# Another issue order of the first stage of a hybrid decoder block: input and state-space input first, memory keys and values last

## The chip, the core and the metric

The kernel runs on one core of one Trainium2 chip. The metric is the device time of one execution in microseconds (us); lower is better. The time before the change is the median of three runs, 1627.50 us (1625.43 to 1628.37).

In what follows PE is TensorE (the matrix engine), DVE is VectorE, ACT is ScalarE, POOL is GpSimd and SP is the sync engine, which here issues every DMA. "L424" is line 424 of the kernel.

## What is computed

One decoder block over 1024 tokens of width 1024 in float32, with a memory of 256 tokens:

```
u = rms_norm(x, norm_mix);  proj = u @ w_in        # splits into u_ssm, q, k, v, f, gates
y_ssm = gelu(s5_ssm(u_ssm));  out_a = glu(y_ssm @ w_glu)
out_b = forgetting_attention(q, k, v, f) @ w_fox_o
h = x + (sigmoid(gate_a)*out_a + sigmoid(gate_b)*out_b) @ w_mix_out
h = h + memory_cross_attention(rms_norm(h), rms_norm(mem), w_mem_q, w_mem_kv, w_mem_o)
h = h + swiglu_ffn(rms_norm(h));  return rms_norm(h)
```

The change touches only the first stage. It makes three things: the normalised input u, turned so that channels lie on partitions; `u_ssm`, the first 512 columns of `proj`; and the keys and values of the memory, `rms_norm(mem) @ w_mem_kv`. None of the three pieces `u_ssm`, keys and values needs another; `u_ssm` is read by the second stage, the keys and values only by the cross-attention, far later.

## The kernel before

**Precision.** Each float32 operand is split into a high and a low part (`split`, L172: a ScalarE cast makes the high part, and VectorE subtracts it from the source for the low part, or GpSimd does where a flag says so). Every product is three matmuls, high by high, high by low and low by high (`mm3`, L161).

**The first stage** (`stage_in`, L327) is a string of steps, `ORDER_IN` (L40). A loop (L437) walks the string and calls one small function per step, so the string is the order in which the instructions are written down. Tokens are handled in tiles of 128: `m` and `n` are the two memory tiles, 0 to 7 the eight tiles of x. The letters are:

- `F t` fetches tile t (512 KB, L344); `G0` and `G1` fetch the gains of the memory norm and the input norm, spread over all partitions (L348). All share eight buffers of the tag `xt`.
- `Q t` squares and sums a tile on ScalarE (L353). `R` makes the reciprocal root (L182): for a pair of x tiles it is eleven small VectorE instructions, for a memory tile one of them is on GpSimd. `S t` scales the tile (L212 on VectorE; with a `g`, L209 on ScalarE and L210 on GpSimd).
- `T t b` turns half a tile by four TensorE transposes (L218); `E t b` splits the result into high and low parts of u or of the memory (L173, L174).
- `D i` fetches weight block i (512 KB, L377): 0 to 3 are the columns of the keys, 4 to 7 rows of the values, 8, 9, a and b the four column blocks of `w_in` that give `u_ssm`. `W i` splits it. There are two raw buffers and four pairs of split buffers, in rotation: a fetch waits until an earlier split has read its buffer, a split until an earlier product has used its pair.
- `K h` and `k h` are the product and the split of one head's keys (24 matmuls of 256 columns), `V` and `v` the same for the values (4 times 12 matmuls of 512 columns, all four into two PSUM banks). When they are done, they are stored in DRAM (`kv_d`, L396 and L411).
- `U q h` is one of eight products of `u_ssm` (24 matmuls of 512 columns): column block q for half h of the tokens. Half 0 needs x tiles 0 to 3, half 1 tiles 4 to 7. `u q h` copies the result out (L421) and, after half 1, stores it by eight DMAs to `u_d` (L424).
- `L0` issues the fourteen small loads of the state-space parameters (L1028 to L1046), `L1` turns them (L1048 to L1059). `P` is one piece of the tables made from them (`prepare`, L1061), nearly all VectorE.
- `X24` is 24 matmuls on the identity, to warm TensorE up (L231).

The tiles of `us` and of the keys and values share four buffers (tag `kv`). All tiles of the stage lie in a pool called `xin`, which is given back when the stage is written down; the second stage's pool, `qp`, is placed where it lay (L312 to L315).

**The second stage** (`stage_ssm`, L441) interleaves 32 gate products (24 matmuls of 512 columns each, two to a 512 KB weight block of `w_in`, L149) with the state-space work of four groups of channels. For each group: `weights` (L1157) makes power tables on GpSimd and VectorE (it begins at L1175 and ends with the doubling steps of L1207 to L1209), `turn_weights` (L1217) turns them on TensorE (L1224, L1230) and places them by seven DMAs, `states` (L1241) reads `u_d`, multiplies (L1252) and scans on VectorE, `out` (L1284) multiplies (L1294, L1295) and takes the gelu on ScalarE (L1298). The first group's `turn_weights` stands before the fifth gate product, its `out` before the tenth.

**What sets the order.** The program is written down in the order above, but each engine's queue is drawn up at build time by the framework's planner. It ranks instructions by the order of writing and may let a later one pass an earlier one that it expects to be waiting. Within a queue the hardware runs in order: an engine whose first instruction waits holds up those behind it. SP's queue holds all DMA issues.

Of the kernel before, what the change touches and what calls it, by code (L numbers as in the profile page):

```python
# [37 lines left out]
RSLOT_LATE = (0, 1, 2, 3, 4, 4, 5, 5, 6, 6, 7, 7)  # L38

ORDER_IN = """  # L40
G0 Fm Qm Fn D1 X24 Qn Rm D0 Sm F1 G1 Tm0 Rn Em0 Sn Tn0 F0 Tm1 W0 Q0 Tn1 En0 F2 Q1 W1g En1 Em1 K0 D2 F3 K1 R0
S0 T00 T01 k0 E00 Q2 W2g D3 E01 D4 S1 T10 Q3 W3 k1 D5 K3 K2 W4 E10 W5 D6 R1 k2 T11 k3 S2 F4 Q4 V0 F5 S3g T30
E11 D7 Q5 F7 T20 R2 T21 E21 E20 S4 E30 W6 W7 T40 V1 D8 S5 E40 W8 T31 V2 L0 T41 E31 V3 D9 Db T50 F6 Q6 v T51 W9
E51 U00 Da Q7 L1 E41 u00 R3 S6 Wa T60 E50 S7 T61 T70 Wbg E61 U10 E60 P0 U20 u10 T71 E70 E71 u20 P1 U21 U11 U30
P2 u30 U31 u11 u31 U01 u21 P3 P4 P5 u01
"""


# [1614 lines left out]
```

## Time and profile before

| | us |
|---|---|
| median of three runs | 1627.50 |
| the profiled execution's own time | 1627.33 |
| its span, first to last instruction | 1625.6 |
| TensorE busy in the span | 1548.8 |
| TensorE's first matmul of the gates (second stage) | 111.53 |
| TensorE's last work of the second stage | about 328 |
| mean granted TensorE clock | 0.976 |

The profile is of one execution. Its span is 1.7 us shorter than the execution's time. A row of the time line gives the start, the length, the engine, the line and operation, what it writes and reads and, in brackets, the idle time of the engine ahead of it and what ended it. A row of stretches gives, for each, its length, each engine's busy time with the number of instructions, the granted TensorE clock (1.00 is full speed), the busy share of the DMA engines and GB/s. A row of waits reads "who <- for whom: us in total, times, longest".

### The profile page before, as it was taken

To read this page: it belongs to the slowest core of one execution; us is meant where nothing else is said; L and a number is where in the kernel's file an instruction comes from. 1 tells how busy PE (TensorE), PEld (TensorE's weight loads), DVE (VectorE), ACT (ScalarE), POOL (GpSimd) and SP (SyncE) were. 2 spreads that over 40 slices of the span, in tenths; PEclk is the share of its full clock that TensorE was granted. 3 is DMA by queue.
4 is the path that set the end of the run, shared out by engine and by line. 5 is a ranking of instruction groups with operands and counts; after the bars stand their busy time and mean duration, and the time that the engine had idled before them with its cause. 6 is when DMAs were issued, how large, how long until landed. Compare 5 with 4: busy or idle time off the path is not lost.

```text
span 1625.6 us, 20551 instructions
## 1 busy us (share of the span) xinstructions
PE 1548.8 (95%) x7313; PEld 1271.5 (78%) x7313; DVE 1022.2 (63%) x1850; ACT 646.4 (40%) x1169; POOL 257.2 (16%) x339
## 2 busy tenths in 40 slices
PE   7799599999899989999999989999999999899997
PEld 6588588899677768888888777888888888688886
DVE  6645554514678786764355698767666776555555
ACT  6322233322566654222235565333333333244342
POOL 2107465100111112310001210001000000000001
PEclk8899899999899999999999999999999999899999
DMA  7655567742321463544303145444554454795642
GB/s 262 124 87 103 52 123 128 144 85 32 50 54 47 118 163 94 166 130 143 91 12 102 56 182 188 149 155 158 164 169 151 160 164 160 263 380 193 196 156 104
DMA packets 226102, 221.77 MB, mean 136 GB/s; under 512 B 50872, under 2 KB 159512, under 8 KB 226000
## 3 DMA queue, kind: packets, MB, share of 16 engines
q1 hardware_dynamic: 226000, 220.47, 48.2%
q8 instruction: 57, 0.93, 0.2%
q14 instruction: 45, 0.37, 0.1%
HBM read 154.06 MB, written 64.32 MB: 134 GB/s over the span
## 4 chain that ended last, share of the span: by engine, by line
PE 77%; DVE 9%; DMA 6%; ACT 3%; POOL 2%; issue 2%; SPq 0%; POOLq 0%; DVEq 0%; ACTq 0%
PE mm L766 14%; PE mm L163 7%; PE mm L164 7%; PE mm L165 7%; PE pv L766 7%; PE mm L905 4%; PE sc L905 3%; PE sc L766 3%; PE sc L163 3%; PE sc L164 3%; PE sc L165 3%; PE pv L905 3%; DMA raw<-in_w_in_dram 2%; PE misc L905 2%; DVE wlo L174 1%
## 5 line engine op out<-in xcount | busy, mean ns | idle before, releaser
L174 DVE TENSOR_TENSOR wlo<-raw,whi 128x1024 fp32r<-128x1024 f32 (+2 forms) x126 | 133.6, 1062 | 190.4 <-ACT whi L173 178.1
L173 ACT CAST whi<-raw 128x1024 fp32r<-128x1024 f32 (+2 forms) x129 | 116.0, 903 | 302.5 <-DMA raw<-in_w_in_dram 79.0
L163 PE MATMUL mm<-uh,whi 128*128 128x512 f32 x344 | 140.3, 408 | 0.3 <-DVE mc L1482 0.3
L165 PE MATMUL mm<-uh,wlo 128*128 128x512 f32 x344 | 138.0, 401 | 0.0
L164 PE MATMUL mm<-ul,whi 128*128 128x512 f32 x344 | 137.7, 400 | 0.0
L174 DVE TENSOR_TENSOR ol<-or,oh 128x1024 fp32r<-128x1024 f32 x73 | 88.7, 1224 | 72.9 <-ACT oh L173 72.5
L173 ACT CAST oh<-or 128x1024 fp32r<-128x1024 f32 x73 | 76.8, 1053 | 107.0 <-PE pv L905 40.5
L798 POOL TENSOR_TENSOR g<-a,c 128x512 f32<-128x512 f32 x22 | 35.3, 1606 | 390.2 <-ACT a L797 390.2
L165 PEld LDWEIGHTS mm<-uh,wlo 128*128 128x128 f32 x344 | 66.6, 193 | 13.7 <-DVE wlo L174 0.2
L163 PEld LDWEIGHTS mm<-uh,whi 128*128 128x128 f32 x344 | 67.1, 195 | 13.0 <-DVE mc L1482 0.6
L164 PEld LDWEIGHTS mm<-ul,whi 128*128 128x128 f32 x344 | 66.9, 194 | 11.8
L192 POOL TENSOR_TENSOR r<-ms,mhalf 128x1 f32<-128x1 f32 x26 | 17.4, 671 | 369.2 <-DVE ms L188 360.7
L1514 POOL TENSOR_TENSOR pl<-pf,ph 128x512 fp32r<-128x512 f32 (+1 forms) x32 | 36.9, 1152 | 235.8 <-DVE ph L1513 221.9
L1511 ACT ACTIVATE pf<-sc 128x512 f32<-128x512 f32 (+1 forms) x96 | 46.3, 489 | 49.1 <-DVE sc L1507 34.1
L766 PE MATMUL pv<-S3h,we 128*128 128x512 f32 x176 | 58.2, 390 | 1.0 <-ACT S3h L173 1.0
L905 PE MATMUL mm<-oh 128*128 128x512 f32 x106 | 41.5, 391 | 0.0
L905 PE MATMUL mm<-ol,oh 128*128 128x512 f32 x106 | 41.5, 391 | 0.0
L905 PE MATMUL mm<-oh,ol 128*128 128x512 f32 x106 | 41.5, 391 | 0.0
L1517 DVE TENSOR_TENSOR pl<-pf,ph 128x512 fp32r<-128x512 f32 (+2 forms) x64 | 36.4, 571 | 7.8 <-ACT ph L1516 7.2
L165 PE MATMUL sc<-uh,wlo 128*128 128x512 f32 x104 | 40.6, 390 | 0.5 <-DVE wlo L174 0.5
L163 PE MATMUL sc<-uh,whi 128*128 128x512 f32 x104 | 40.8, 393 | 0.0
L163 PE MATMUL mm<-yh,whi 128*128 128x512 f32 x104 | 40.8, 392 | 0.0
(574 smaller groups left out, 4553.5 us busy)
## 6 DMA issues: line engine op xcount, KB each, us to landing
or<-c_d SPq DMA_DIRECT2D x77, 256.0 KB
raw<-in_w_ffn_in_dram SPq DMA_DIRECT2D x22, 512.0 KB
rawb<-in_w_ffn_in_dram SPq DMA_DIRECT2D x22, 512.0 KB
wo<-in_w_ffn_out_dram SPq DMA_DIRECT2D x22, 512.0 KB
c_d<-g SPq DMA_DIRECT2D x44, 256.0 KB
t_d<-wo SPq DMA_DIRECT2D x44, 256.0 KB
or<-t_d SPq DMA_DIRECT2D x44, 256.0 KB
raw<-in_w_in_dram SPq DMA_DIRECT2D x20, 512.0 KB
```

The lines of the kernel that those rows point to most:

```text
L163: T.matmul(ps, lh, rh, start=first, stop=False)
L164: T.matmul(ps, lh, rl, start=False, stop=False)
L165: T.matmul(ps, ll, rh, start=False, stop=last)
L173: self.A.copy(hi, src)
L174: (self.G if pool_lo else self.V).tensor_sub(lo, src, f32(hi))
L192: self.G.tensor_tensor(out=r, in0=v, in1=self.mhalf[:, 0:n], op=ALU.pow)
L766: T.matmul(ps, l_[:, k, :], r_, start=first and k == 0 and i == 0, stop=k == 3 and i == 2, skip_group_check=True)
L798: G.tensor_mul(g[:, 512:], a1, c1)
L905: T.matmul(ps, l_[:, gi], r_[:, 512:], start=n < 3 and p == 0 and k == 0 or n == 7 and p == 0 and k == 0, stop=p == NP - 1 and k == 2, ski ...
L1511: A.activation(pf[:, off:], ps[:, off:], AF.Exp)
L1514: G.tensor_sub(pl[:, off:], pf[:, off:], f32(ph[:, off:]))
L1517: V.tensor_sub(pl[:, off:], pf[:, off:], f32(ph[:, off:]))
```

## The change

Only the string changes; each step is in both, once, with the same flags but for two weight blocks (1 and 2), whose low parts go from GpSimd to VectorE.

```diff
 ORDER_IN = """
-G0 Fm Qm Fn D1 X24 Qn Rm D0 Sm F1 G1 Tm0 Rn Em0 Sn Tn0 F0 Tm1 W0 Q0 Tn1 En0 F2 Q1 W1g En1 Em1 K0 D2 F3 K1 R0
-S0 T00 T01 k0 E00 Q2 W2g D3 E01 D4 S1 T10 Q3 W3 k1 D5 K3 K2 W4 E10 W5 D6 R1 k2 T11 k3 S2 F4 Q4 V0 F5 S3g T30
-E11 D7 Q5 F7 T20 R2 T21 E21 E20 S4 E30 W6 W7 T40 V1 D8 S5 E40 W8 T31 V2 L0 T41 E31 V3 D9 Db T50 F6 Q6 v T51 W9
-E51 U00 Da Q7 L1 E41 u00 R3 S6 Wa T60 E50 S7 T61 T70 Wbg E61 U10 E60 P0 U20 u10 T71 E70 E71 u20 P1 U21 U11 U30
-P2 u30 U31 u11 u31 U01 u21 P3 P4 P5 u01
+F0 F1 G1 X24 F2 F3 D8 Q0 Q1 R0 F4 F5 S0 T00 E00 T01 F6 E01 S1 D9 T10 E10 T11 E11 Q2 Q3 R1 S2 T20 W8 E20 T21 E21 F7
+S3g T30 E30 T31 E31 Q4 Q5 R2 U00 Da S4 T40 E40 W9 T41 E41 S5 T50 E50 T51 E51 U10 u00 Q6 Q7 R3 Db S6 T60 E60 T61 E61
+Wa L0 S7 T70 E70 T71 E71 U20 u10 Fm Fn G0 Wbg U30 u20 L1 D0 U01 u30 P0 D1 u01 W0 Qm Qn Rm Sm U11 u11 P1 W1 Tm0 Em0
+Tm1 Em1 D2 P2 U21 u21 W2 Rn Sn P3 Tn0 En0 Tn1 En1 D3 P4 U31 u31 P5 W3 D4 K0 k0 D5 K1 k1 W4 D6 K2 k2 W5 D7 K3 k3 W6
+V0 W7 V1 V2 V3 v
 """
```

In the new string x is fetched, normalised and turned first, with the eight products of `u_ssm` following as their tiles and weights come (first half 0 of all four blocks, then half 1). The memory tiles are fetched behind them, and the four key products and the four value products end the stage. `us` is stored before the keys and values are computed, and the stage's last stores are those of the keys and values.

## The prediction

> **What bounds the kernel now.** I read the page first, then the table of stretches, then TensorE's waits, then the chain of waits around its largest gap.
>
> ```profile
> span 1625.6 us, 20551 instructions
> PE 1548.8 (95%) x7313; PEld 1271.5 (78%) x7313; DVE 1022.2 (63%) x1850; ACT 646.4 (40%) x1169; POOL 257.2 (16%) x339
> ```
> ```profile
> core 0: us, PE busy (x) PEld busy (x) DVE busy (x) ACT busy (x) POOL busy (x), PEclk, DMA share, GB/s
> 0.00:53.10 53.10, 39.03 (x225) 32.32 (x225) 34.59 (x86) 29.61 (x55) 11.84 (x15) 0.90 0.75 228
> 53.10:111.50 58.40, 52.27 (x221) 42.41 (x222) 37.47 (x159) 16.33 (x31) 4.13 (x1) 0.91 0.53 98
> 111.50:175.00 63.50, 59.54 (x291) 50.49 (x290) 32.56 (x36) 16.00 (x26) 41.15 (x85) 0.97 0.51 97
> 175.00:199.00 24.00, 11.12 (x49) 8.59 (x48) 12.03 (x17) 4.10 (x6) 8.45 (x15) 0.83 0.62 55
> 199.00:328.00 129.00, 129.00 (x646) 110.42 (x647) 66.54 (x93) 47.19 (x79) 54.07 (x103) 0.97 0.71 129
> ```
> TensorE (PE) is the bound: 1548.8 of 1625.6 us. Its missing 76.8 us lie partly here: 53.10+58.40−39.03−52.27 = 20.2 us before 111.5, where the gates' matmuls start, 4.0 us up to 175, 12.9 us up to 199, and none from there to 328. So a reordered first stage can win only at these gaps, and slow clock beside them (0.90 and 0.91 granted).
>
> ```profile
> PE pv L1224 <- ACT m L1298: 12.4, 1, 12.4
> PE misc L218 <- DVE ul L174: 3.6, 2, 3.3
> PE misc L218 <- DVE xt L212: 3.0, 1, 3.0
> ```
> ```profile
> 91.35 25.79 SPq L424 DMA_DIRECT2D u_d<-us  x32
> 119.34 0.99 POOL L1175 TENSOR_TENSOR w<-ld_re,bb_re 128x448 f32<-128x448 f32 x1 [41.02 <-DMA u_d<-us]
> ```
> ```profile
> 180.09 1.15 DVE wlo L174
> 181.25 13.54 DMA raw<-in_w_in_dram
> 198.21 0.61 ACT m L1298
> 198.95 1.94 PE pv L1224 x8
> ```
> The second fence is the key. GpSimd's first instruction on the state-space tables (L1175) sat idle 41.0 us and ran at 119.34, when the last store of `us` had landed: the second stage's tiles lie where the first stage's lay, so its table chain starts only when the first stage's last tile is free. The third fence is the end of that chain: tables, scans, a late weight split, a load of 13.54 us, ScalarE's gelu, and TensorE back at 198.95. Tables to restart is 198.95−119.34 = 79.6 us. TensorE stands idle before that restart and is full after it, so **the start of the table chain, not the start of the gates, carries to the end.** What I must find is when it starts after the change.
>
> **The change, part by part.** 140 steps change places; none is added or removed. Two weight splits (W1, W2) move their low part from GpSimd to VectorE, 2×1.22 us by the row below, which I cost at nothing: they fall under U, where TensorE has 43 us of work and VectorE only waits to serve it; without that cover they would delay K by as much. The work of the stage goes: x tiles and norms, state-space input U (8 products), memory K (4) and V (4). The sum follows TensorE to the end of V, then the last store.
>
> *DMA supply.* Rows of ScalarE, each released by a load:
> ```profile
> 6.61 1.06 ACT L353 ACTIVATE junk<-xt 128x1024 bf16<-128x1024 f32 x1 [4.53 <-DMA xt<-in_mem_dram]
> 8.02 1.06 ACT L353 ACTIVATE junk<-xt 128x1024 bf16<-128x1024 f32 x1 [0.27 <-DMA xt<-in_mem_dram]
> 152.46 1.05 ACT L173 CAST whi<-raw 128x1024 fp32r<-128x1024 f32 x1 [6.86 <-DMA raw<-in_w_in_dram]
> 158.39 1.05 ACT L173 CAST whi<-raw 128x1024 fp32r<-128x1024 f32 x1 [4.88 <-DMA raw<-in_w_in_dram]
> ```
> The second and third 512 KB of the queue landed at 6.61 and 8.02: 1.4 us per tile of 4 KB rows. Two 512 KB blocks of `w_in` (512-byte pieces) landed 5.93 us apart: four times slower. New queue: F0 at 5.2, F1 6.6, G1 8.0, F2 9.4, F3 10.8, D8 16.7, F4 to F6 by 20.9, D9 26.8, F7 28.2, Da 34.1, Db 40.0 (estimates from those two spacings). The Trainium skill's DMA: Bandwidth & Descriptors, Specifications, puts line rate at pieces of 512 B and more; by it all four blocks would be there about 18 us sooner and the 3 us stall below would go (1617.3). The trace disagrees, and I go by 5.93.
>
> *Start of U.* U00 needs tiles 0 to 3 turned and W8 split. VectorE's prices:
> ```profile
> 17.69 0.17 DVE L190 TENSOR_SCALAR ms<-ss 128x2 f32<-128x2 f32 x1 [0.35 <-ACT junk L353]
> 19.86 2.48 DVE L212 SCALAR_TENSOR_TENSOR xt<-xt,r,gain 128x1024 f32<-128x1024 f32 x2
> ```
> ```profile
> L174 DVE TENSOR_TENSOR wlo<-raw,whi 128x1024 fp32r<-128x1024 f32 x11 | 13.5, 1223 | 11.9 <-ACT whi L173 11.9
> L174 DVE TENSOR_TENSOR ul<-misc,uh 128x256 fp32r<-128x256 f32 x16 | 6.7, 419 | 0.1
> L174 POOL TENSOR_TENSOR wlo<-raw,whi 128x1024 fp32r<-128x1024 f32 x3 | 10.6, 3529 | 45.7 <-ACT whi L173 45.7
> ```
> A pair's root took 19.86−17.69 = 2.17 us, a scaling 1.24, a quarter tile's low part 0.42, a weight split 1.22. Two roots, three scalings (the fourth is GpSimd's), 16 low parts and one split are 4.3+3.7+6.7+1.2 = 15.9 us. They begin when F1 is squared, 6.6+1.3 = 7.9. So U00 starts at **24** (bounds 20, if short gaps overlap, and 30, if each tile's TensorE, ScalarE, VectorE round trip is exposed).
>
> *TensorE's work from there.*
> ```profile
> 100.42 0.39 PE L165 MATMUL mm<-uh,wlo 128*128 128x512 f32 x1
> 111.30 0.39 PE L165 MATMUL mm<-uh,wlo 128*128 128x512 f32 x1
> 23.00 0.28 PE L165 MATMUL mm<-mh,wlo 128*128 128x256 f32 x1
> 24.06 0.28 PE L165 MATMUL mm<-mh,wlo 128*128 128x256 f32 x1
> 54.97 0.63 PE L163 MATMUL mm<-uh,whi 128*128 128x512 f32 x1
> 57.10 0.63 PE L165 MATMUL mm<-uh,wlo 128*128 128x512 f32 x1
> 37.70 0.60 PE L218 MATMUL misc<-ident,xt 128*128 128x128 f32 x4
> ```
> From 100.42 to 111.30 are 48 matmuls: 0.227 us each at full clock; the narrow ones 9 in 1.06, 0.118 each; cold ones (54.97 to 57.10) 5 in 2.13, 0.43 each. U is 8×24×0.227 = 43.5 us; K 96×0.118 = 11.3; V 48×0.227 = 10.9. Twelve groups of four transposes (x tiles 4 to 7, memory) at 0.4 (0.60 less the overlap with the next matmul) are 4.8, the state-space loads' five small ones 1.3. A cold start, as at 53.95 to 57.5, costs 10×(0.43−0.23) = 2.0, because TensorE has only scattered transposes to do after its 24 warm-up matmuls. TensorE: Matmul & The Clock Gate in the Trainium skill, Part 4, says that transposes do not count as busy for the clock; by that those 2.0 us are certain, and if transposes did keep the clock the result would be 1618.3; no row here isolates it.
>
> *Weights.* W9 is ready at 26.8+2.2 = 29 and Wa at 36.3, before U10 and U20 need them (about 32 and 37.5). Db at 40.0 plus 1.05 of ScalarE plus 3.53 of GpSimd gives 44.6 against about 44: up to 1 us. The small state-space loads are free to slip ahead of Db:
> ```profile
> 33.03 0.80 SPq L1039 DMA_DIRECT2D craw<-in_c_re_dram  x1
> 38.22 0.43 SPq L377 DMA_DIRECT2D raw<-in_w_mem_kv_dram  x1
> 39.80 4.26 SPq L1039 DMA_DIRECT2D craw<-in_c_re_dram  x3
> 44.10 3.96 SPq L1039 DMA_DIRECT2D craw<-in_c_im_dram  x4
> ```
> Seven of them held the queue 8.2 us. I take 3 us for the stall, from 0 to 8. End of U: 24+43.5+2.0+4.8+1.3+3.0 = **78.6**. W0 to W3 have landed by then, since U01 to U31 free their slots one by one 5.4 us apart. K and V: 22.2 plus 2 for weights just in time, so V ends at **102.8** (111.5 ended U before, with K and V behind it already).
>
> *The last store.* New: the last tiles of the stage are V's, split (two casts, two subtractions, 2.0 us) and stored by two 512 KB DMAs after V, where `us` stores lie under K and V. How long these take to land, no row shows there: from below, the last `us` store, whose row ends at 117.14, had landed by 119.34, 2.2 us; from above 5.9 of a gate weight ahead in the queue plus 2×1.4 plus 2.2 = 10.9. I take 7.5, nearer the upper, because gate weights are fetched in that very stretch. The table chain starts at 102.8+2.0+7.5 = **112.3** against 119.3: 7.0 us sooner.
>
> *Sum.* 1627.33 (the profiled execution; its span 1625.6 and 1.7 around it) − 7.0 = **1620.3**. The median, 1627.50, is the same to 0.2. The gates start 8.7 us sooner but gain nothing of their own: the 16.9 us of gaps from 111.5 to 199 go on ending with the table chain, 79.6 us after its start. All later stages keep their order and shift as one.
>
> **The rivals.**
> *Slower: V's weights arrive one by one.* The sync engine's issues leave in order, and 32 `us` stores, each set of eight waiting for a U, now stand among D2 to D7.
> ```profile
> 10.98 1.99 ACT L173 CAST whi<-raw 128x1024 fp32r<-128x1024 f32 x2 [1.80 <-DMA raw<-in_w_mem_kv_dram]
> 43.18 1.05 ACT L173 CAST whi<-raw 128x1024 fp32r<-128x1024 f32 x1 [1.06 <-DMA raw<-in_w_mem_kv_dram]
> ```
> In before, eight key and value blocks took 43.18−10.98 = 32.2 us from first to last cast, with two raw buffers and nothing of `us` between. At that pace, plus 1.2 for the last split and 2.7 for the last product, K and V last 36.1 instead of 24.2: +11.9, the chain starts at 124.2, and the time is 1627.3+4.9 = **1632.2**. It decides once K and V last over 31.2 us. Against it: four of the eight are loaded under U.
>
> *No change: the state-space loads go ahead of Db.* The planner already let them pass a weight (the fetch at 38.22 stands ahead of them in the order string, yet the load at 33.03 left before it). 8.2 us ahead of Db instead of 3, and another cold start of 2.0: +7.2, **1627.5**. So the written order need not be the order of the queues.
>
> *The second gap closes.* ScalarE's cast for a late weight stood ahead of gelu; if the planner, from another start, puts gelu first, the 12.4 us wait goes: **1607.9**. For it: the next three groups show no such gap (129.0 of 129.0 busy). Against: chain and gates stand nearly as before to each other, 9.5 us apart instead of 7.8.
>
> **How the numbers follow.** Forecast 1620.3, chance 0.40; its own range 1614 to 1626. Slower rival 0.30, no change 0.15, gap closed 0.15. Faster or slower by 0.2% is 3.3 us, about what a measurement here can tell from none. Faster: 0.37+0.15 = 0.52; same: 0.03 of the forecast, 0.02 of the slower rival and 0.11 of the unchanged one, 0.16; slower: 0.28+0.04 = 0.32. The bounds move the forecast by −4 to +6 (start of U), −3 to +5 (stall), −5.3 to +3.4 (store). For 8 in 10 the range is 1606 to 1637: from just under the closed gap to 5 over the slower rival.
>
> **What would show it.** U's first matmul near 24 and its last near 79, the fourth product waiting on a weight by some 3 us; K and V in one run to about 103; L1175 near 112, released by a store of keys and values; TensorE's restart 79.6 us behind it; full from there. Wrong if L1175 is released by something else or its distance to the restart changes, if a cast for D4 to D7 stalls ScalarE with TensorE waiting, or if stages after 328 of before differ in length by more than 2 us.

## The result, and the profile after

The changed kernel takes 1641.44 us in the median of six runs (1638.11 to 1645.01), the kernel before 1627.58 beside it: ratio 1.0079, 95% interval 1.0062 to 1.0097. It is 13.9 us slower, where 7.2 us faster was forecast. The profiled execution of after took 1645.01, the longest of the six, so its later positions are up to 3.6 us late. Of all executions in this document one stood far out, 8734 us, in the run "woven, tables first": its ratio leaves it out, and its median is 1627.38 without it.

The page of after, its head (us, share of the span, instructions):

```profile
span 1643.2 us, 20562 instructions
...
PE 1553.7 (95%) x7313; PEld 1274.2 (78%) x7313; DVE 1018.8 (62%) x1852; ACT 646.6 (39%) x1169; POOL 250.9 (15%) x337
```

TensorE's idle time grew from 76.8 to 89.5 us. Here is the first stage of after cut at its own marks: the first product of U, the first of K, the last of V, the first of the gates.

```profile
core 0: us, PE busy (x) PEld busy (x) DVE busy (x) ACT busy (x) POOL busy (x), PEclk, DMA share, GB/s
0.00:39.78 39.78, 13.93 (x60) 10.61 (x60) 20.03 (x60) 19.68 (x37) 4.49 (x12) 0.67 0.74 179
39.78:93.31 53.53, 52.23 (x242) 42.50 (x242) 41.86 (x171) 15.82 (x34) 4.28 (x3) 0.96 0.45 104
93.31:128.40 35.09, 28.83 (x145) 24.35 (x143) 10.15 (x13) 7.96 (x11) 0.00 (x0) 0.85 0.49 124
128.40:134.47 6.07, 0.12 (x1) 0.00 (x1) 0.02 (x1) 1.10 (x2) 0.00 (x0) 0.90 0.46 98
```

U began at 39.78, not 24; it lasted 53.5 us, as forecast (54.6); K and V lasted 35.1, not 24.2, at a granted clock of 0.85; and the gates waited 6.1 us for their first weight. The row on which the forecast turned, GpSimd's first instruction on the tables, and the row of ScalarE that tells what let it go (the tables' tiles lie where the keys' and values' lay):

```profile
146.52 0.62 ACT L1213 COPY r<-R 128x512 f32<-128x512 f32 x1 [1.60 <-DMA kv_d<-kv]
```
```profile
146.79 0.99 POOL L1175 TENSOR_TENSOR w<-ld_re,bb_re 128x448 f32<-128x448 f32 x1 [93.20 <-DMA raw<-in_w_in_dram]
```

So the chain starts 27.5 us later than before (119.34) and 34.5 later than forecast (112.3): 15.8 at the start of U, 10.9 in K and V, 8.9 between V's end and the chain (18.4 for 9.5), less 1.1 in U. Yet the end moved only half as far. TensorE's waits after the first stage in after, with the last gate's sigmoid (L453, first to last start) of both kernels, before first:

```profile
PE pv L1294 <- DMA Tt<-W: 5.0, 1, 5.0
PE pv L1295 <- DVE St L1281: 4.0, 2, 3.7
...
PE pv L1252 <- ACT F L1225: 1.2, 1, 1.2
```
```profile
L453 ACT ACTIVATE gs<-mm x19: 588/597/620, 122.6 to 342.8; 128x512 f32<-128x512 f32 x19
```
```profile
L453 ACT ACTIVATE gs<-mm x19: 591/599/602, 153.7 to 358.4; 128x512 f32<-128x512 f32 x19
```

The 12.4 us for the gelu (L1298) is gone. From the chain's start to the last sigmoid it is 211.6 us (358.4−146.8), where before had 223.5. Slower by 27.5, shorter by 11.9: 15.6 us, and 13.9 by the medians.

### The profile page after: what moved, and what is told of

The parts are those of the page before. It is cut to its first block, busy times and chain, and to the rows that moved or that the text cites. A ratio compares the mean times of both kernels' runs of the same rounds, so it can differ in the third digit from the quotient of the medians.

```text
span 1643.2 us, 20562 instructions
## 1 busy us (share of the span) xinstructions
PE 1553.7 (95%) x7313; PEld 1274.2 (78%) x7313; DVE 1018.8 (62%) x1852; ACT 646.6 (39%) x1169; POOL 250.9 (15%) x337
## 4 chain that ended last, share of the span: by engine, by line
PE 76%; DVE 8%; DMA 6%; ACT 3%; POOL 3%; issue 2%; SPq 1%; POOLq 0%; DVEq 0%; ACTq 0%
PE mm L766 14%; PE pv L766 7%; PE mm L163 7%; PE mm L165 7%; PE mm L164 7%; PE mm L905 4%; PE sc L905 3%; PE sc L766 3%; DMA raw<-in_w_in_dram 3%; PE sc L163 3%; PE sc L165 3%; PE sc L164 3%; PE pv L905 3%; PE misc L905 2%; DVE wlo L174 1%
## 5 line engine op out<-in xcount | busy, mean ns | idle before, releaser
L174 DVE TENSOR_TENSOR wlo<-raw,whi 128x512 fp32r<-128x512 f32 (+2 forms) x128 | 133.9, 1049 | 172.2 <-ACT whi L173 164.9
L164 PE MATMUL sc<-ul,whi 128*128 128x512 f32 x104 | 41.0, 394 | 0.0
```

Source lines behind the costliest of these rows:

```text
L164: T.matmul(ps, lh, rl, start=False, stop=False)
L174: (self.G if pool_lo else self.V).tensor_sub(lo, src, f32(hi))
```

## The experiments

All runs in one table. "Chain" is the first instruction of L1175, or what stands on that line; +9.9 and +19.8 are the repeats that were added behind it. The ratio is to the kernel before on the same chip.

| run | median us | ratio, 95% | U00 | chain | last sigmoid | chain to sigmoid |
|---|---|---|---|---|---|---|
| before | 1627.58 | | 53.95 | 119.3 | 342.8 | 223.5 |
| after | 1641.44 | 1.0079 (1.0062–1.0097) | 39.78 | 146.8 | 358.4 | 211.6 |
| W8 late | 1641.92 | 1.0075 (1.0059–1.0091) | 40.41 | 145.5 | 357.0 | 211.5 |
| D8, W8 late | 1639.83 | 1.0059 (1.0044–1.0074) | 31.16 | 142.8 | 354.6 | 211.8 |
| key copies on VectorE | 1640.10 | 1.0075 (1.0055–1.0096) | 40.19 | 143.6 | 355.1 | 211.5 |
| key and value weights as rows | 1640.65 | 1.0070 (1.0055–1.0085) | 39.65 | 142.5 | 354.7 | 212.2 |
| three queues | 1634.39 | 1.0044 (1.0027–1.0060) | 40.98 | 136.8 | 348.9 | 212.1 |
| three queues, D8 late | 1630.67 | 1.0017 (1.0006–1.0028) | 31.70 | 131.9 | 343.0 | 211.1 |
| value stores by GpSimd | 1644.00 | 1.0101 (1.0081–1.0121) | 40.37 | 148.5 | 360.0 | 211.5 |
| woven | 1631.21 | 1.0013 (1.0003–1.0022) | 33.49 | 133.4 | 347.1 | 213.7 |
| woven, tables first | 1627.65 | 1.0000 (0.9989–1.0011) | 34.38 | 132.0 | 345.7 | 213.7 |
| after, chain +9.9 | 1649.47 | 1.0131 (1.0115–1.0148) | 39.51 | 142.7+9.9 | 362.7 | 210.1 |
| before, chain +9.9 | 1624.20 | 0.9968 (0.9955–0.9981) | 54.12 | 120.1+9.9 | 338.5 | 208.5 |
| before, chain +19.8 | 1632.04 | 1.0025 (1.0015–1.0035) | 54.76 | 119.8+19.8 | 346.3 | 206.7 |
| before, one low part on GpSimd | 1623.92 | 0.9969 (0.9958–0.9981) | 53.87 | 120.1 | 337.0 | 216.9 |

Positions in one execution scatter, and this bears on small differences in the table. In "after, chain +9.9" nothing of the first stage was changed, yet its chain starts 4.1 us sooner than in the profile of after (142.7 for 146.8), and its keys and values last 33.4 us for 35.1, at a granted clock of 0.91 in place of 0.84 from K's first product to V's. So a chain that starts 4 us sooner, or keys and values that are 2 us shorter, are not clear of this scatter by themselves.

### The start of U

In after, rows of ScalarE, VectorE and TensorE show why U00 came late:

```profile
9.56 1.06 ACT L353 ACTIVATE junk<-xt 128x1024 bf16<-128x1024 f32 x1 [2.48 <-DMA xt<-in_x_dram]
...
18.65 1.04 ACT L173 CAST whi<-raw 128x1024 fp32r<-128x1024 f32 x1 [6.65 <-DMA raw<-in_w_in_dram]
```
```profile
13.22 0.16 DVE L197 SCALAR_TENSOR_TENSOR rt<-rt,ms 128x2 f32<-128x2 f32 x1
19.73 1.23 DVE L174 TENSOR_TENSOR wlo<-raw,whi 128x1024 fp32r<-128x1024 f32 x1 [6.35 <-ACT whi L173]
20.87 0.15 DVE L198 SCALAR_TENSOR_TENSOR r<-rt,r 128x2 f32<-128x2 f32 x1
```
```profile
25.92 1.09 PE L218 MATMUL misc<-ident,xt 128*128 128x128 f32 x4 [12.48 <-DVE rt L196]
...
39.78 1.65 PE L163 MATMUL mm<-uh,whi 128*128 128x512 f32 x3 [3.33 <-ACT uh L173]
```

The root of tiles 2 and 3 is cut in two: VectorE stands 6.35 us before the low part of the first w_in block, whose load lands at 18.65, and the rest of the root waits behind it. The first run writes that split later.

```diff
-F0 F1 G1 X24 F2 F3 D8 Q0 Q1 R0 F4 F5 S0 T00 E00 T01 F6 E01 S1 D9 T10 E10 T11 E11 Q2 Q3 R1 S2 T20 W8 E20 T21 E21 F7
-S3g T30 E30 T31 E31 Q4 Q5 R2 U00 Da S4 T40 E40 W9 T41 E41 S5 T50 E50 T51 E51 U10 u00 Q6 Q7 R3 Db S6 T60 E60 T61 E61
+F0 F1 G1 X24 F2 F3 D8 Q0 Q1 R0 F4 F5 S0 T00 E00 T01 F6 E01 S1 D9 T10 E10 T11 E11 Q2 Q3 R1 S2 T20 E20 T21 E21 F7 S3g
+T30 E30 T31 E31 Q4 Q5 R2 W8 U00 Da S4 T40 E40 W9 T41 E41 S5 T50 E50 T51 E51 U10 u00 Q6 Q7 R3 Db S6 T60 E60 T61 E61
```

> The changed kernel with one step moved: W8, the split of the first block of w_in, is written just ahead of U00 in place of between the tiles' turns. Theory (queue order): the split's cast (18.65) and subtraction (19.73) stand in the two engines' queues behind a block that lands at 18.65, and hold up the tiles' roots and casts by about 6 us each; without that U00 starts at 26 to 32 instead of 39.78, and what is gained there is still there when the gates start (134.5 less 8 to 13). Rival (supply): the block itself, 5.9 us in the queue ahead of tiles 4 to 7, sets the start; then U00 stays within 3 us of 39.78. If the gates' start carries to the end the time is 1641.4 less 8 to 13, about 1631; if it does not, about 1641.

It changed nothing: U00 at 40.41, and the same stall in the same place.

```profile
12.97 0.16 DVE L197 SCALAR_TENSOR_TENSOR rt<-rt,ms 128x2 f32<-128x2 f32 x1
19.99 1.22 DVE L174 TENSOR_TENSOR wlo<-raw,whi 128x1024 fp32r<-128x1024 f32 x1 [6.86 <-ACT whi L173]
```

The planner put the split where it had been, twelve steps ahead of its place in the string. So this run says nothing for or against the theory; it shows that the written order is not the queue's order. The second run moves the load too, with this for the first line of the string:

```diff
-F0 F1 G1 X24 F2 F3 D8 Q0 Q1 R0 F4 F5 S0 T00 E00 T01 F6 E01 S1 D9 T10 E10 T11 E11 Q2 Q3 R1 S2 T20 E20 T21 E21 F7 S3g
+F0 F1 G1 X24 F2 F3 Q0 Q1 R0 F4 F5 S0 T00 E00 T01 F6 D8 E01 S1 D9 T10 E10 T11 E11 Q2 Q3 R1 S2 T20 E20 T21 E21 F7 S3g
```

> As the run with W8 late, and D8, the fetch of that block, is written behind the fetch of tile 6 instead of ahead of tile 4. Theory (queue order): little beyond the other run, U00 within 3 us of it, since its last piece then is the block itself (tiles 0 to 6 by about 13, the block by about 19). Rival (supply): tiles 4 to 6 come 5.9 us sooner and U00 and U's later products go that much sooner, U ends about 6 us before the other run's.

```profile
31.16 1.39 PE L163 MATMUL mm<-uh,whi 128*128 128x512 f32 x3 [1.85 <-ACT uh L173]
```

U00 began 8.6 us sooner, K's first product 2.95 sooner (90.36 for 93.31), and the chain 4.0 (142.8 for 146.8). Neither forecast fits: U00 came 9.3 us ahead of the run before this, not within 3, and U ended 2.6 ahead of it, not 6. The stall is gone, the root of tiles 2 and 3 now runs from 11.46 to 13.6 without a break, so the block's place in the queue of loads was the cause of 8.6 us of the late start, through the split that waits for it; 5.7 of the 8.6 us were given back inside U. What is left at the chain and in the time lies within the scatter here; the pair of runs with three queues, below, shows it clearly.

### Keys and values

TensorE's stretch of K in after, and ScalarE in it:

```profile
93.30:113.20 19.90, 15.55 (x97) 14.42 (x95) 4.92 (x8) 3.59 (x6) 0.00 (x0) 0.83 0.36 91
```
```profile
99.11 0.37 ACT L173 CAST kv<-mm 128x256 fp32r<-128x256 f32 x1 [2.38 <-PE mm L165]
99.38 1.05 ACT L173 CAST whi<-raw 128x1024 fp32r<-128x1024 f32 x1
106.16 0.37 ACT L173 CAST kv<-mm 128x256 fp32r<-128x256 f32 x1 [5.73 <-PE mm L165]
106.43 1.05 ACT L173 CAST whi<-raw 128x1024 fp32r<-128x1024 f32 x1
113.21 0.37 ACT L173 CAST kv<-mm 128x256 fp32r<-128x256 f32 x1 [5.74 <-PE mm L165]
```

Each cast of a weight block (whi) stands behind the copy of a key product (kv) that is still running; so TensorE, done with that product, waits for the cast and its low part, here those of the third key block (W2):

```profile
100.48 0.38 PE L163 MATMUL mm<-mh,whi 128*128 128x256 f32 x1 [1.41 <-ACT whi L173]
...
101.74 0.39 PE L165 MATMUL mm<-mh,wlo 128*128 128x256 f32 x1 [0.76 <-DVE wlo L174]
```

Two runs take one suspect each.

```diff
-        B.split(kv[0][:, cs], kv[1][:, cs], ps.pop(("k", h))[:, :ML])
+        src = ps.pop(("k", h))[:, :ML]
+        B.V.tensor_copy(kv[0][:, cs], src)
+        B.V.tensor_sub(kv[1][:, cs], src, f32(kv[0][:, cs]))
```

> The changed kernel, with the high part of the four key results copied out by VectorE in place of ScalarE (the values as before). Theory (ScalarE's order): in the changed kernel a copy that waits for its product (2.4 to 5.7 us each) stands ahead of the cast of the next key block, so TensorE waits for that cast and its subtraction (three times 2.2 us) and runs cold after it; without the copies on ScalarE the casts run ahead, the eight blocks take under 29 us in place of 35.1, time 1634 to 1638. Rival (weight supply): the casts then wait for their loads instead, 35 us stay, time within 2 us of 1641.4. Second rival: VectorE's copies stand ahead of the subtractions in the same way; again no change.

```diff
-        if i < 4:
-            src = w_mem_kv[:, i * P:(i + 1) * P]
-        elif i < 8:
-            src = w_mem_kv[2 * (i - 4) * P:2 * (i - 3) * P, 512:1024]
+        if i < 8:
+            src = w_mem_kv[i * P:(i + 1) * P, :]
```

> The changed kernel, where each of the eight weight blocks of the memory is fetched as 128 whole rows of 4 KB in place of 512-byte or 2-KB pieces, so the products use wrong weights; bytes and instructions are the same in number. Theory (ScalarE's order): K stays as long as it was (19.8 us from first product to the first value product) since its casts waited for products, not for loads; only the one cast of a value block that waited 5.3 us for its load comes sooner, time 1636 to 1641. Rival (weight supply): blocks land 1.4 us apart in place of about 4, K and V take about 24 us, the gates start 11 us sooner, time about 1630.

K and V lasted 32.9 us in the first (not 33.5, as the next expectation counts) and 32.6 in the second, for 35.1; neither time differs from after beyond the intervals, and set beside the 33.4 us of "after, chain +9.9" less than 1 us of either is clear of the scatter. In the second, K lasted 19.6 us to the first value product, as its theory said, so the loads are not what holds K. In the first, VectorE now did what ScalarE had done, its second rival:

```profile
98.30 0.42 DVE L394 CAST kv<-mm 128x256 fp32r<-128x256 f32 x1 [2.38 <-PE mm L165]
98.70 0.76 DVE L395 TENSOR_TENSOR kv<-mm,kv 128x256 fp32r<-128x256 f32 x2
99.37 1.22 DVE L174 TENSOR_TENSOR wlo<-raw,whi 128x1024 fp32r<-128x1024 f32 x1
```

The copy waits for the product, and the next block's low part (wlo) stands behind the copy. That gave the next run: copies on VectorE as above, casts on ScalarE, low parts on GpSimd, three queues of which none holds a split behind a product.

```diff
-Tm1 Em1 D2 P2 U21 u21 W2 Rn Sn P3 Tn0 En0 Tn1 En1 D3 P4 U31 u31 P5 W3 D4 K0 k0 D5 K1 k1 W4 D6 K2 k2 W5 D7 K3 k3 W6
-V0 W7 V1 V2 V3 v
+Tm1 Em1 D2 P2 U21 u21 W2g Rn Sn P3 Tn0 En0 Tn1 En1 D3 P4 U31 u31 P5 W3g D4 K0 k0 D5 K1 k1 W4g D6 K2 k2 W5g D7 K3 k3
+W6g V0 W7g V1 V2 V3 v
```

> The changed kernel with the three jobs of keys and values on three engines: the key copies on VectorE (as in the run with the key copies there), the low parts of the weight blocks 2 to 7 on GpSimd, which is idle there, the casts alone on ScalarE. Theory (two in-order queues, not one): moving the copies to VectorE won only 1.6 us because each copy, waiting for its product, then stood ahead of the next block's low part; with the low parts on GpSimd nothing that waits for a product stands ahead of a split. K and V then last 26 to 29 us in place of 35.1, with a clock near 1.00, the table chain starts 6 to 9 us sooner than 146.8, time 1632 to 1636. Rival (supply, two raw buffers and some 4 us per block): the casts wait for loads instead, 33 to 35 us stay, time 1640 to 1643.

The two stretches of it, K and V:

```profile
93.50:104.86 11.36, 11.36 (x98) 11.26 (x96) 3.62 (x9) 3.53 (x4) 4.83 (x3) 1.00 0.62 155
104.86:122.74 17.88, 13.60 (x49) 9.77 (x48) 0.85 (x2) 3.14 (x3) 9.31 (x4) 0.90 0.65 157
```
```profile
103.66 1.05 ACT L173 CAST whi<-raw 128x1024 fp32r<-128x1024 f32 x1 [7.47 <-DMA raw<-in_w_mem_kv_dram]
```

K took 11.4 us, the forecast's 11.3, at full clock, where after had 19.9. V took 17.9, where after had 15.2: with the queues clear its casts wait for loads. Together 29.2, the time 7.1 us lower by the medians and 5.7 by the ratios. So in K the order in the two queues was the cause, and in V the supply is the next bound. Low parts on GpSimd without the copies on VectorE were not tried. The last run of this kind puts D8 late as well:

> The same, with the fetch of the first w_in block behind tile 6 and its split just ahead of U00, as in the second run of all. There U00 began 8.6 us sooner but the key products only 3.0. Theory: the two gains add, the chain starts 3 to 4 us ahead of the run without this, time 2 to 4 us below it. Rival: what is won at the start is lost in waits for later tiles or blocks, the same time within 1.5 us.

The chain started 4.9 us sooner and the time fell by 3.7 (4.4 by the ratios): the gains add. Together they take the ratio from 1.0079 to 1.0017.

Two runs give K and V cover in place of queues. The woven order computes them between U's products:

```diff
+F0 F1 G1 X24 F2 F3 F4 Q0 Q1 R0 F5 F6 D8 S0 T00 T01 S1 E00 E01 T10 T11 Q2 Q3 R1 E10 E11 F7 D9 S2 T20 T21 S3g E20 E21
+T30 T31 E30 E31 Q4 Q5 R2 W8 U00 Fm Fn G0 S4 T40 E40 T41 E41 W9 S5 T50 E50 T51 E51 U10 u00 Q6 Q7 R3 D0 S6 T60 E60
+T61 E61 S7 T70 E70 T71 E71 u10 U01 D1 Qm Qn Rm Rn u01 W0 Sm Tm0 Em0 Tm1 Em1 U11 Sn Tn0 En0 Tn1 En1 u11 W1 Da K0 k0
+D2 K1 k1 L0 Wa W2 D3 U20 W3 D4 K2 k2 W4 D5 K3 k3 u20 L1 D6 V0 U21 u21 W5 P0 D7 V1 W6 P1 Db V2 W7 P2 V3 v Wbg P3 U30
+u30 P4 U31 u31 P5
```

> Tiles of x first as in the changed kernel, but the four key and four value products are written between the products of U, the stores of us come last, and W8 is late. Theory (no cover): the 35.1 us that keys and values lasted at the end (24 forecast) came from their own in-order chain of cast, product and copy with nothing beside it; woven between U's products that loss of about 11 us goes, the gates' first weight is there in time (6 us more), and the start is as in the run with W8 late; gates at 105 to 118, time 1615 to 1628. Rival (weight supply): eight blocks at about 4 us each with two raw buffers are needed within the same stretch wherever the products stand; then TensorE waits for them between U's products too and the time stays above 1632.

```profile
94.41 0.58 PE L165 MATMUL mm<-mh,wlo 128*128 128x256 f32 x1 [9.33 <-DVE wlo L174]
```

The ratio fell to 1.0013, and the time lies between the theory's and the rival's. D8 is late here too, so what the cover alone gave is not told apart. One wait is left in K: this low part waited behind the tables (P) in VectorE's queue. So the tables were written ahead of the keys, L0 behind D0 and L1 with the pieces from U01 on (`... R3 D0 L0 S6 ... U01 L1 D1 P0 ...`):

> The woven order once more, with the state-space loads and the pieces of the tables moved ahead of the key products, under the second half of U's tiles, where VectorE had little to do. Theory: the 9.3 us that TensorE waited in the woven order for the low part of a key block (VectorE worked on the tables from 83.5 to 93.1 with that subtraction behind them) goes, the gates start 6 to 10 us sooner than in the woven order, time 1621 to 1626, below the kernel before. Rival: the planner puts the tables where it will, or the loads of the tables delay the memory's blocks; then within 3 us of 1631.2.

That gave 3.6 us more by the medians, 2.1 by the ratios, and the time of the kernel before, not less: the wait of 9.3 us went, but the chain started only 1.4 us sooner (132.0). What held the rest was not taken apart.

### From V's end to the chain

After V (128.40), in after, ScalarE and SP:

```profile
133.37 1.04 ACT L173 CAST whi<-raw 128x1024 fp32r<-128x1024 f32 x1 [10.24 <-DMA raw<-in_w_in_dram]
134.32 0.58 ACT L173 CAST kv<-sc 128x512 fp32r<-128x512 f32 x1
134.95 1.05 ACT L173 CAST whi<-raw 128x1024 fp32r<-128x1024 f32 x1
135.90 0.58 ACT L173 CAST kv<-sc 128x512 fp32r<-128x512 f32 x1
```
```profile
136.51 2.53 SPq L411 DMA_DIRECT2D kv_d<-kv  x2
139.13 7.46 SPq L149 DMA_DIRECT2D raw<-in_w_in_dram  x2
```

The copy of the finished values stands behind the cast of a gate weight that waits for its load; the two stores follow at 136.5 and 138.0, and the last has landed when ScalarE goes on at 146.52.

```diff
-            B.split(kv[2][:, cs], kv[3][:, cs], ps.pop(("v", t)))
+            src = ps.pop(("v", t))
+            B.V.tensor_copy(kv[2][:, cs], src)
+            B.V.tensor_sub(kv[3][:, cs], src, f32(kv[2][:, cs]))
         for i in range(2, 4):
-            S.dma_start(kv_d[i], f32(kv[i]))
+            B.G.dma_start(kv_d[i], f32(kv[i]))
```

> The changed kernel, with the values copied out by VectorE in place of ScalarE and their two stores issued by GpSimd's queue in place of the sync engine's. Theory: in the changed kernel the copy of the values stands in ScalarE's queue behind a gate weight's cast that waits 10 us for its load, and the two stores (136.51) behind three fetches of gate weights (123.09 to 136.07); with other queues the stores leave some 2 to 4 us after that copy could be made, the table chain starts at 136 to 140 in place of 146.8, and by the one to one step the time is 1630 to 1635. Rival: the stores' transfers are what takes the time, among the gate weights in the same DMA engines; then the chain starts within 3 us of 146.8 and the time stays within 3 us of 1641.4. Second rival: VectorE's queue holds the same gate weight's subtraction in front of the copy; then some 3 us are won at most.

The time and the chain are the first rival's, and the rows show the second rival's mechanism: VectorE had the same gate weight's low part (134.30) ahead of the copies' last pieces (135.44 to 138.5), and GpSimd's stores left at 137.04 and 138.77, no sooner than in after. So the run does not tell what sooner stores would have won. They landed late:

```profile
137.04 0.77 POOL L413 DMA_DIRECT2D kv_d<-kv  x1 [82.84 <-DVE kv L410]
138.77 0.54 POOL L413 DMA_DIRECT2D kv_d<-kv  x1 [0.97 <-DVE kv L411]
```
```profile
DMA to landing us min/median/max: 7.2/8.3/9.3
```

A store of 512 KB took 7.2 and 9.3 us there, among the gate weights; in after, from the sync engine's queue, the last took 8.5 (138.0 to 146.5). What would happen if the copy did not stand behind the cast was not tried by itself.

### From the chain to the end

GpSimd's first instruction for group 0, repeated, delays the chain and leaves the gates where they are:

```diff
-            G.tensor_tensor(out=w1v, in0=bpow(self.ld[0], 7), in1=bvec(self.bb[bx], 7), op=ALU.mult)
+            for _ in range(11 if q == 0 and o == 0 else 1):
+                G.tensor_tensor(out=w1v, in0=bpow(self.ld[0], 7), in1=bvec(self.bb[bx], 7), op=ALU.mult)
```

> The kernel before with GpSimd's first instruction on the tables of group 0 (128x448, 0.99 us) carried out eleven times instead of once, the result unchanged: the table chain is ready 9.9 us later, while the gates start where they did. The prediction's step (the chain carries one to one): 1627.5 plus 9.9, about 1637.4. Rival (slack): the order in which the second stage's queues are drawn up leaves room, so that less than half of it, under 5 us, reaches the end.

> The changed kernel with the first GpSimd instruction of group 0's tables carried out eleven times, the result unchanged: its table chain is ready 9.9 us later, the gates start where they did. The prediction's step (one to one): about 1651. The theory that has taken its place (the gates' start is what carries, the chain only fills or opens gaps of some 5 us by the place of single instructions in the queues): within 5 us of 1641.4.

> The kernel before with the first GpSimd instruction of group 0's tables carried out 21 times, the result unchanged: its table chain is ready 20 us later. With 11 times the second stage's 12.4 us gap had closed and the time was 1624.2. Theory (once that gap is closed the chain carries one to one): 10 us over that, 1632 to 1636. Rival (slack): the chain has room, within 4 us of 1624.

(The third has 21 in the loop.) In after the delay of 9.9 us cost 8.0. In before the first 9.9 us made the kernel faster, by 0.3%, which neither theory had; the next 9.9 cost 7.8 by the medians and 9.3 by the ratios. So a delay of the chain alone costs 0.8 to 0.94 of the time that GpSimd was given to do, and my theory after the first four runs, that the gates' start alone carries, fell. The share itself is loose. The planner set other small steps between the repeats, so the tables moved by more than 9.9 us: in after their first sum (fre) by 14.3 against the chain's start, group 0's last product (L1187) by 11.0. Set against 14.3, the 8.0 us are 0.56. In before and in the run with 21 repeats that sum stands at these places, and in the second TensorE waited for it:

```profile
121.60 1.16 POOL L1177 TENSOR_TENSOR fre<-w,w 128x448 f32<-128x448 f32 x1
```
```profile
151.00 1.13 POOL L1178 TENSOR_TENSOR fre<-w,w 128x448 f32<-128x448 f32 x1
```
```profile
PE pv L1225 <- POOL fre L1178: 11.2, 1, 11.2
```

In after itself there is slack at this point: the sums were done at 155.55, and TensorE took them up at 159.22 without a wait. One to one is therefore not shown, only that a good part of a delay reaches the end. The one thing apart is before itself: with the first delay its gap for the gelu was gone, as in after. Another run takes that gap away and leaves the chain's start:

```diff
-            w[j] = B.wblock(w_in, 0, 8, C_G + j * P, P)
+            w[j] = B.wblock(w_in, 0, 8, C_G + j * P, P, j == 5)
```

> The kernel before, with the low part of one gate weight block (the sixth, cast at 152.46) made by GpSimd in place of VectorE. Theory: the 12.4 us gap of the kernel before starts with that low part, which stood in VectorE's queue behind the doubling steps until 180.01; it held a raw buffer, so the fetch of the eighth block left at 181.25, its cast waited till 194.87, and the gelu stood behind the cast. With GpSimd doing it in its own idle time (159.8 to 164.6) the fetch leaves 15 us sooner and the gap goes, while the table chain starts at 119.3 as before: 1627.5 less 9 to 12.4, or 1615 to 1618.5. Rival: the gap belongs to the start of the chain (119.3) and not to that block; then the wait only changes its name and the time is 1626 to 1629.

ScalarE and TensorE's waits of it:

```profile
176.36 1.04 ACT L173 CAST whi<-raw 128x1024 fp32r<-128x1024 f32 x1 [7.71 <-DMA raw<-in_w_in_dram]
...
179.70 1.09 ACT L1298 ACTIVATE m<-pv 128x512 f32<-128x512 f32 x2
```
```profile
PE pv L1252 <- ACT F L1225: 5.7, 1, 5.7
PE pv L1295 <- DVE St L1281: 5.6, 2, 5.4
```

The cast came at 176.36 for 194.87, the gelu at 179.70 for 198.21, and the 12.4 us wait is gone: its cause is shown to be the low part that stood in VectorE's queue and held a raw buffer. But 7.3 us of other waits took its place: 5.7 for the next group's tables, and 5.6 where before had 4.0. The kernel is 0.3% faster than before, less than expected; this run and before with the delay of 9.9 are the two that beat both kernels.

## Why the prediction was wrong

**"U00 starts at 24 (bounds 20 … and 30)": failed, 39.78.** The step added up VectorE's work as if nothing in its queue could wait for a load. It had the load right (D8 at 16.7; it landed at 18.65) and the split's price right (1.23 us), but took the split as one more 1.2 us and not as a place where the queue stands until 19.73. That is 8.6 of the 15.8 us (D8 late); the rest no run took apart. The Trainium skill's DMA: Bandwidth & Descriptors, Specifications, with line rate from 512 B up, would have had that block at 12.4 (an estimate: 9.56 for tile 2, and two spacings of 1.4); the landing at 18.65 speaks against it.

**"U 43.5 + 2.0 + 4.8 + 1.3 + 3.0": held in sum**, 53.5 for 54.6. TensorE was busy 52.2 us for the 51.6 of the first four terms. The stall of 3.0 for Db did not come (1.3 us of waits, none for a weight), because U started so late that its weights were there: that term was not put to the test.

**"K and V: 22.2 plus 2": failed, 35.1.** The 2 us for weights just in time are the term. The split of W2, priced at nothing because it would fall under U, was cast only at 99.38, in K, behind the copy of the second key product, and TensorE waited 2.2 us for it; two more such waits followed. TensorE was busy 28.8 us, 6.6 over its 22.2 at full clock, and idle 6.3; each wait was followed by matmuls at a lower clock. The slower rival had 36.1 for the same term, near the measured 35.1 by luck, since its cause was another: one block after the other through the loads. With fast loads 32.6 were left (33.4 with nothing changed, in "after, chain +9.9"), with clear queues 29.2.

**"The last store": failed, 18.4 for 9.5.** The landing, 10.0 for 7.5, lay inside its bounds. What failed was "two casts, two subtractions, 2.0 us" behind V: the last copy was made at 135.9, 7.5 us after V, since the next stage's first cast stood ahead of it. That is read from the rows; the one run on it did not clear the place.

**"Tables to restart is 79.6 us", one to one: half right.** Over the ten kernels with x first and no added delay, the chain's start moved from 131.9 to 148.5 and the time from it to the last sigmoid stayed at 211.1 to 213.7. The gates' start moved along with it in most of them, so this alone does not tell which of the two carries; two pairs do. From woven to woven with the tables first, the first sigmoid of the gates came 4.2 us sooner (133.87 for 138.03), the chain 1.4 and the last sigmoid 1.4. From after to the value stores by GpSimd, the gates began within 0.2 us of each other (134.32 for 134.47), the chain 1.7 later and the last sigmoid 1.6 later. Both times the end went with the chain, by small amounts in one execution each; alone, a delay of the chain cost 0.8 to 0.94 of GpSimd's added work, or less by the tables' own places. But this constant is 12 us shorter than in before, because the gap for the gelu went. The prediction had read the late weight split before that gap as a part of the chain; the run with that low part on GpSimd left the chain's start at 120.1, and the gap was gone. That the gap closes was the third rival, chance 0.15 and price 12.4, and it came true; why it closed in after no run took apart. The mistake was to set the rivals against each other: the slower one's place and the third one's gap came in the same kernel. As a rough estimate, 27.5 later at 0.8 to 1.0, less 5 to 13 for the gap (0.31% in the run with the low part on GpSimd; 5.2 and the 8 of the delay itself in the first delay of before), is 9 to 22 us slower; measured 13.9.

**The cause.** Shown, for the start of U and for K: in the first stage of after, splits of weights stand in the same in-order queues as the roots of tiles and the copies of results, and wait there for a load or another engine. Clearing these two places took the ratio from 1.0079 to 1.0017. Argued, not shown by itself: that keys and values pay for such waits because at the end of the stage no product of U covers them; the woven orders, which give cover again, came to 1.0013 and 1.0000, but with the late D8 among their changes. Open: the rest of the start, and how much of the 18.4 us would go if the values' copy stood ahead of the gates' cast.

## What to carry to other kernels

When a step is moved to the end of a stage, look for what its engine queues hold next to it: a copy that waits for a product ahead of the next split, or the next stage's first cast ahead of the last copy, costs more than the work. A bound for a start time must count the latest load that anything in the queue waits for, not only the work in it. And two mechanisms of which one makes the kernel slower and one faster are no alternatives: price them together.

## What was not expected of the hardware

GpSimd's low part of a 128x1024 weight took 3.53 us in before (mean of three) and 2.4 here, in the run with three queues:

```profile
95.31 4.75 POOL L174 TENSOR_TENSOR wlo<-raw,whi 128x1024 fp32r<-128x1024 f32 x2 [43.16 <-ACT whi L173]
```

VectorE was little used in that stretch (3.62 of 11.36 us); whether that is why was not tried. In after, though, it took 2.38 with VectorE counted as busy for 2.15 of them, 1.83 in one small instruction (128x2) of the kind that took 0.17 elsewhere; so a VectorE that counts as busy is not enough to make it slow. A store of 512 KB took 7.2 to 9.3 us from issue to landing beside loads of w_in. And short waits cost twice: in after TensorE stood idle for 4.4 of K's 19.9 us and lost 4.2 more at a clock of 0.83 (15.55 busy for 11.3), which the run with three queues had back in full. How much such a wait costs is not fixed: in "after, chain +9.9", with the same waits, K's matmuls were busy for 14.0 us and lost 2.6.
